# Attention pipeline of an encoder trunk: query turns moved two steps ahead, scores issued ahead of values, another first term, pieces at other steps

## The chip, the cores and the metric

The kernel is one program on 1 core of one Trainium2 chip. The metric is the device time of one execution in microseconds (us). Engines are named as in the profile: PE is TensorE's matmuls, PEld its weight loads, DVE is VectorE, ACT is ScalarE, POOL is GpSimd, SP is SyncE.

## The reference, cut to what matters

Two sequences of 512 and 256 tokens (768 in all, 6 blocks of 128) pass through two layers with shared weights. A layer is a half-weighted gated feed-forward, a mixer, and a second half-weighted feed-forward, each on a normalised input and each added to the running x. The mixer of layer 0 is a gated linear recurrence. The mixer of layer 1 is windowed attention with 16 query heads on 4 key heads, and the change is in this one:

```
qb = q.reshape(B, nb, L, Hk, G, d)                       # blocks of L=128 queries, G=4 heads per key head
s = einsum('bnqhgd,bnkhd->bnhgqk', qb, kband) * d**-0.5  # keys: the block, one before, one after
m = maximum(max(s), sink);  p = exp(s - m)
denom = sum(p) + exp(sink - m)
o = einsum('bnhgqk,bnkhd->bnqhgd', p / denom, vband)     # then o @ w_o
```

All inputs and outputs are float32. A product of float32 matrices is made of three products of the engine's faster float32 format: each operand is split into a high and a low part, and high*high, high*low and low*high are summed in PSUM.

## The kernel before, in words

**The whole.** `tile_trunk_kernel` runs feed-forward f0, the recurrence `hgrn`, feed-forwards f1 and f2, the attention `swa`, and f3. The products of the feed-forwards use a seven-product scheme for 2x2 blocks (L423, L498). Instructions are recorded in the order of the Python calls, and a scheduler then sets the order on each engine from that order, from the tiles that an instruction needs, and from when it reckons that these are ready. Each engine works through its own queue strictly in that order and waits on semaphores.

**The attention stage.** `swa` first projects keys and values for all blocks. The query projection is cut into pieces by the generator `proj_tok`: a query block of 512 columns takes 24 matmuls (L263, L264, L265) and is handed out in four pieces of six. After the fourth, `put_q` copies it out of PSUM (ACT, L970) and rotates 16 of every 64 columns (DVE, L973, L975, L976, L977). `q0` holds the queries of key heads 0 and 1, `q1` those of 2 and 3. Half of the output projection, `wo`, is cut into pieces in the same way.

**Units.** The attention is 24 units, numbered 0 to 23 here: 4 key heads, and for each the 6 query blocks, with all 4 query heads of one key head in a unit. Units with number 1 or 2 modulo 6 have three key blocks (384 keys), the others two (256 keys). A unit goes through these methods of `Unit`:

- `turn`: two PE transposes of the query block (L1155), then `split` into a high part by a copy on ACT (L268, tile tA) and a low part by a subtraction on DVE (L269, tile tA). The low part needs the high one.
- `scores`: 12 matmuls (L1169), three terms for each of 4 heads, with 64 of the 128 array rows each, two side by side; into 4 PSUM banks.
- `maxima`: four DVE instructions (L1185) that add the band mask and give the row maximum.
- `sink` and `exps`: DVE L1204; ACT exponentials with row sums (L1198) and that of the sink (L1205).
- `denominator`: DVE L1210, L1211, then the scaling of the four heads' probabilities (L1214).
- `probs`: per key block four PE transposes (L1221) and a copy by ACT (L1223, tile tA).
- `values`: matmuls (L1230) into 64 of the 128 array columns each; a source-level matmul here is two instructions on the engine.
- `finish`: a split of the result, ACT L268 and DVE L269 on tile big, the input of the output projection.

[...]

**What sets the order.** `pipeline` collects events with a step and a rank, sorts them by both, and calls them. Unit i has its section at step 4i: the matmuls of `values` of unit i-2 and of `scores` of unit i, tied into one chain with `issue_after`, then `finish` of unit i-2 and `maxima` of unit i. `turn` of unit i stands at step 4i-1 with rank 5 (the first at -5), the exponentials and the denominator at 4i with rank 2, the transposes of its probabilities at 4i+5 and on. The pieces come with rank 3 at the steps in the list `extra`: 16 query pieces (the last four blocks of `q0`), 25 more (`q1`), the reload of x, and 24 pieces of `wo`.

Of the kernel before, what the change touches and what calls it, by code (L numbers as in the profile page):

```python
# [48 lines left out]
class Trunk:  # L49
# [932 lines left out]
    def swa(self, next_row):  # L982
# [28 lines left out]
        def put_q(half):  # L1011
            def f(s, b, ps):
                gb = SEQS[s][0] // P + b
                if half and gb % 3 == 0:
                    hold.append(self.big([P, 3, 512]))
                t = hold[gb // 3][:, gb % 3] if half else self.xt()[:, :512]
                self.rotate(ps, 512 // HD, b, t.rearrange("p (h d) -> p h d", d=HD))
                for gg in range(2):
                    qtok[(s, b, half * 2 + gg)] = t[:, gg * 256 : (gg + 1) * 256]

            hold = []
            return f
# [3 lines left out]
        def units(gs):  # L1026
            def alloc(g):
                if g not in of:
                    of[g] = [self.big([P, 2, T], F32R) for _ in range(2)]
                return of[g]  # L1030

            for g in gs:
                for s, (off, n) in enumerate(SEQS):
                    for b in range(n // P):
                        q = lambda s=s, b=b, g=g: qtok[(s, b, g)]
                        yield Unit(self, s, b, g, q, kT, vv, lambda g=g: alloc(g))
# [4 lines left out]
        q = itertools.chain(self.proj_tok("q0", put_q(0)), self.proj_tok("q1", put_q(1)))  # L1041
        wo = self.out_proj("sw_o", 0, act, None)
        for _ in range(8):
            next(q)
        piece = lambda g: lambda: next(g, None)
        extra = [(i * 5 / 4 - 4, piece(q)) for i in range(16)]
        extra += [(18 + 2 * i, piece(q)) for i in range(25)]
        extra.append((46, self.reload_x))
        extra += [(66 + i * 5 / 4, piece(wo)) for i in range(24)]
        self.pipeline(list(units(range(KV))), extra)  # L1050
        self.drain(wo)
        self.drain(self.out_proj("sw_o", 1, act, next_row))
# [42 lines left out]
    def pipeline(self, units, extra):  # L1095
        events = []

        def at(step, rank, *calls):
            events.append((step, rank, len(events), calls))

        last = []

        def tiles(done, new):
            mms = ([] if done is None else done.values()) + ([] if new is None else new.scores())
            for n, mm in enumerate(mms):
                with self.tc.issue_after(last[-1]) if n else nullcontext():
                    last[:] = [mm()]

        def section(done, new):
            tiles(done, new)  # L1110
            if done is not None:
                done.finish()
            if new is not None:
                new.maxima()

        for i in range(len(units) + 2):
            t = 4 * i
            u = units[i] if i < len(units) else None
            done = units[i - 2] if i > 1 else None
            at(t, 1, lambda u=u, done=done: section(done, u))  # L1120
            if u is None:
                continue
            at(t - (1 if i else 5), 5, u.turn)
            at(t, 2, u.sink)
            for h in range(GQ):
                at(t, 2, lambda u=u, h=h: u.exps(h))
            at(t, 2, u.denominator)
            for j in range(u.nkb):
                at(t + 5 + j, 1, lambda u=u, j=j: u.probs(j))
        for step, call in extra:  # L1130
            at(step, 3, call)
        for _, _, _, calls in sorted(events, key=lambda e: e[:3]):
            for c in calls:
                c()


class Unit:
# [22 lines left out]
    def scores(self):  # L1160
        k, nc = self.k, self.k.nc
        self.sc = k.big([P, GQ, 3 * P])
        self.nm, self.den, self.sk = (k.stat(GQ) for _ in range(3))
        self.pss = [k.ps(self.nk) for _ in range(GQ)]

        def one(p, j, x, y, par):
            rows = slice(par * HD, (par + 1) * HD)
            q = self.qT[x][rows, p * P : (p + 1) * P]
            return nc.tensor.matmul(  # L1169
                self.pss[2 * p + par], q, self.kT[y][rows, self.keys], start=j == 0, stop=j == 2  # L1170
            ).ins

        terms = list(enumerate(((0, 0), (0, 1), (1, 0))))
        return [
            lambda p=p, j=j, x=x, y=y, par=par: one(p, j, x, y, par)
            for p in range(GQ // 2)
            for j, (x, y) in terms
            for par in range(2)
        ]
# [178 lines left out]
```

## Time and profile before

| what | value |
|---|---|
| time, median of 3 runs | 2759.03 us (2758.95 to 2759.92) |
| the profiled execution's own time | 2760.57 us |
| its span, first to last instruction | 2758.8 us |
| mean granted TensorE clock | 0.998 |
| busy share of the span: PE, DVE, ACT, POOL | 99%, 76%, 48%, 11% |
| first `scores` matmul to last `values` matmul | 2046.4 to 2226.2 us |

The profile of one execution has a page (engine totals, the span in 40 slices, the chain of work that ended last, the costliest groups of instructions) and views on the trace: the timeline of one engine in a stretch, tables of busy time by stretch, waits by who released whom. In a timeline row the first number is the start in us from the span's beginning, the second how long the row lasted; `x8` merges eight like instructions, and a bracket gives idle time of the engine ahead of the row and what ended it. PE matmuls overlap, so a matmul that "lasts" 0.39 us may be followed 0.23 us after its start by the next: the cost of a group on PE is read from its start to the start of the next group.

### The profile page before, as it was taken

To read this page: it belongs to the slowest core of one execution; us is meant where nothing else is said; L and a number is where in the kernel's file an instruction comes from. 1 tells how busy PE (TensorE), PEld (TensorE's weight loads), DVE (VectorE), ACT (ScalarE), POOL (GpSimd) and SP (SyncE) were. 2 spreads that over 40 slices of the span, in tenths; PEclk is the share of its full clock that TensorE was granted. 3 is DMA by queue.
4 is the path that set the end of the run, shared out by engine and by line. 5 is a ranking of instruction groups with operands and counts; after the bars stand their busy time and mean duration, and the time that the engine had idled before them with its cause. 6 is when DMAs were issued, how large, how long until landed. Compare 5 with 4: busy or idle time off the path is not lost.

```text
span 2758.8 us, 44483 instructions
## 1 busy us (share of the span) xinstructions
PE 2733.7 (99%) x17281; PEld 2481.9 (90%) x17281; DVE 2100.5 (76%) x3662; ACT 1327.5 (48%) x2479; POOL 309.2 (11%) x315
## 2 busy tenths in 40 slices
PE   8999999999999999999999999999999999999998
PEld 8999999888888889999999999999886789999997
DVE  7887788557477568787888878888846768788877
ACT  7444444456466354443446444444546654443444
POOL 1111211000000001121111112111000000221110
PEclk9999999999999999999999999999999999999999
DMA  5544554321110324455444355544412123555443
GB/s 161 135 117 118 137 135 118 120 64 41 55 46 25 122 62 109 118 143 135 120 120 106 88 127 138 134 116 120 151 43 77 47 62 81 134 136 130 117 115 107
DMA packets 330117, 291.63 MB, mean 106 GB/s; under 512 B 11609, under 2 KB 257841, under 8 KB 329905
## 3 DMA queue, kind: packets, MB, share of 16 engines
q1 hardware_dynamic: 294064, 212.43, 25.9%
q0 software_dynamic: 31680, 62.93, 13.3%
q10 hardware_dynamic: 4160, 13.42, 1.4%
q8 instruction: 135, 2.21, 0.3%
q14 instruction: 78, 0.63, 0.1%
HBM read 216.39 MB, written 9.44 MB: 82 GB/s over the span
## 4 chain that ended last, share of the span: by engine, by line
PE 95%; DVE 2%; ACT 2%; DMA 1%; issue 0%; DVEq 0%; SPq 0%; ACTq 0%
PE ps L423 41%; PE ps L498 20%; PE ps L263 9%; PE ps L265 9%; PE ps L264 9%; PE ps L694 1%; PE ps L1230 1%; PE ps L1169 1%; PE ps L839 1%; PE ps L1221 1%; PE ps L325 1%; DMA wr<-wr 1%; PE ps L815 0%; DVE x L520 0%; ACT big L328 0%
## 5 line engine op out<-in xcount | busy, mean ns | idle before, releaser
L423 PE MATMUL ps<-big,w 128*128 128x384 f32 x6720 | 1169.2, 334 | 0.0
L423 PEld LDWEIGHTS ps<-big,w 128*128 128x128 f32 x6720 | 1165.9, 188 | 1.6
L204 ACT CAST w<-wr 128x512 fp32r<-128x512 f32 x600 | 415.1, 706 | 707.4 <-DVE wr L218 371.6
L205 DVE TENSOR_TENSOR w<-wr,w 128x512 fp32r<-128x512 f32 (+1 forms) x520 | 448.5, 866 | 180.9 <-ACT w L204 176.0
L498 PE MATMUL ps<-w,big 128*128 128x512 f32 x2520 | 579.0, 390 | 2.0 <-DVE x L520 1.9
L498 PEld LDWEIGHTS ps<-w,big 128*128 128x128 f32 x2520 | 471.0, 188 | 104.8 <-ACT big L268 4.5
L520 DVE SCALAR_TENSOR_TENSOR x<-ps,x 128x512 f32<-128x512 f32 x468 | 303.6, 683 | 10.2 <-PE ps L265 10.0
L146 POOL DMA_DIRECT2D s<-wr x120 | 105.1, 875 | 1662.9 <-DMA wr<-in_ffn_w_dram 804.5
L263 PE MATMUL ps<-w,big 128*128 128x512 f32 x624 | 253.0, 405 | 0.3
L265 PE MATMUL ps<-w,big 128*128 128x512 f32 x624 | 244.8, 392 | 1.0 <-DVE big L332 1.0
L264 PE MATMUL ps<-w,big 128*128 128x512 f32 x624 | 244.8, 392 | 0.0
L268 ACT CAST big<-tA 128x384 fp32r<-128x384 f32 x296 | 148.1, 513 | 162.2 <-DVE tA L458 76.8
L263 PE MATMUL ps<-big,w 128*128 128x384 f32 (+2 forms) x640 | 219.2, 344 | 3.2 <-ACT big L268 1.9
L264 PE MATMUL ps<-big,w 128*128 128x384 f32 (+2 forms) x640 | 216.3, 338 | 0.7 <-DVE big L269 0.6
L265 PE MATMUL ps<-big,w 128*128 128x384 f32 (+2 forms) x640 | 215.5, 337 | 0.0
L269 DVE TENSOR_TENSOR big<-tA,big 128x384 fp32r<-128x384 f32 x296 | 183.9, 632 | 12.9 <-ACT big L268 12.0
L172 DVE TENSOR_TENSOR w<-wr,w 128x1024 fp32r<-128x1024 f32 x92 | 111.9, 1222 | 78.4 <-ACT w L171 72.6
L263 PEld LDWEIGHTS ps<-w,big 128*128 128x128 f32 x624 | 117.5, 188 | 29.3 <-issue 5.6
L205 POOL TENSOR_TENSOR w<-wr,w 128x512 fp32r<-128x512 f32 x80 | 123.3, 1541 | 179.7 <-ACT w L204 155.2
L171 ACT CAST w<-wr 128x1024 fp32r<-128x1024 f32 x92 | 96.5, 1052 | 97.3 <-PE ps L264 77.7
L265 PEld LDWEIGHTS ps<-w,big 128*128 128x128 f32 x624 | 117.4, 188 | 27.7 <-DVE big L332 1.7
L264 PEld LDWEIGHTS ps<-w,big 128*128 128x128 f32 x624 | 117.7, 189 | 21.8 <-issue 0.4
(163 smaller groups left out, 2906.6 us busy)
## 6 DMA issues: line engine op xcount, KB each, us to landing
wr<-in_ffn_w_dram SPq DMA_DIRECT2D x264, 512.0 KB, 3.9
s<-in_ffn_w_dram SPq DMA_DIRECT2D x120, 256.0 KB, 3.3
s<-wr POOLq DMA_DIRECT2D x120, 256.0 KB, 4.6
wr<-wr POOLq DMA_DIRECT2D x80, 256.0 KB, 3.7
wr<-in_hg_w_in_dram SPq DMA_DIRECT2D x40, 512.0 KB, 3.9
wr<-wr POOLq DMA_DIRECT2D x20, 512.0 KB, 4.6
spill<-x ACTq DMA_DIRECT2D x12, 512.0 KB, 2.8
x<-spill ACTq DMA_DIRECT2D x12, 512.0 KB, 3.3
```

The lines of the kernel that those rows point to most:

```text
L146: self.nc.gpsimd.dma_start(out, src, accum_op=ALU.add)
L172: self.nc.vector.tensor_sub(lo, raw, hi.bitcast(F32))
L204: nc.scalar.copy(h, src)
L205: low = (eng or nc.vector).tensor_sub(l, src, h.bitcast(F32)).ins
L263: nc.tensor.matmul(out, a[0], b[0], start=first, stop=False)
L264: nc.tensor.matmul(out, a[0], b[1], start=False, stop=False)
L265: nc.tensor.matmul(out, a[1], b[0], start=False, stop=last)
L268: self.nc.scalar.copy(hi, src)
L269: self.nc.vector.tensor_sub(lo, src, hi.bitcast(F32))
L423: self.nc.tensor.matmul(ps, a[x], b[y], start=first and k == 0 and i == 0, stop=k == 3 and i == 2, skip_group_check=True,)
L498: nc.tensor.matmul(ps, a[x], w[y], start=name == chain and kp == 0 and q == 0, stop=kp == 1 and q == 2, skip_group_check=True,)
L520: self.nc.vector.scalar_tensor_tensor(x, ps, c, x, ALU.mult, ALU.add)
```

## The change

Five edits, all in the attention stage:

1. `turn` of unit i moves from step 4i-1 (rank 5) to step 4i-2 (rank 2).
2. In a section the chain begins with `scores` of the new unit and ends with `values` of the old one, and `maxima` is called before `finish`.
3. In `scores` the term order of (query part, key part) is low*high, high*high, high*low; it was high*high, high*low, low*high. So the first matmul of a unit needs the low part of the query.
4. The first 16 query pieces stand 7/5 of a step apart (5/4 before), the next 25 begin at step 19 (18 before).
5. The 24 pieces of `wo` stand 7/5 of a step apart (5/4 before).

```diff
-        extra = [(i * 5 / 4 - 4, piece(q)) for i in range(16)]
-        extra += [(18 + 2 * i, piece(q)) for i in range(25)]
+        extra = [(i * 7 / 5 - 4, piece(q)) for i in range(16)]
+        extra += [(19 + 2 * i, piece(q)) for i in range(25)]
         extra.append((46, self.reload_x))
-        extra += [(66 + i * 5 / 4, piece(wo)) for i in range(24)]
+        extra += [(66 + i * 7 / 5, piece(wo)) for i in range(24)]
...
-            mms = ([] if done is None else done.values()) + ([] if new is None else new.scores())
+            mms = ([] if new is None else new.scores()) + ([] if done is None else done.values())
...
             tiles(done, new)
+            if new is not None:
+                new.maxima()
             if done is not None:
                 done.finish()
-            if new is not None:
-                new.maxima()
...
-            at(t - (1 if i else 5), 5, u.turn)
+            at(t - (2 if i else 5), 2, u.turn)
...
-        terms = list(enumerate(((0, 0), (0, 1), (1, 0))))
+        terms = list(enumerate(((1, 0), (0, 0), (0, 1))))
```

What the scheduler makes of it is seen at three places. **First, PE between unit 11 and unit 13.** Before, the turn of unit 12 (L1155), the values of unit 10 (L1230), three projection matmuls, and the first seven of the twelve score matmuls of unit 12 (L1169):

```order
L1155 MATMUL ps_2723_20272<-ident_r_84,big_2625_19823 128x128 x2
L1230 MATMUL ps_2725_20278<-tA_2714_20245,big_2447_18825 64x256 x2
L1230 MATMUL ps_2725_20278<-tA_2716_20252,big_2447_18825 64x256 x2
L263 MATMUL ps_2701_20178<-w_2576_19601,big_2422_18734 128x512
L264 MATMUL ps_2701_20178<-w_2577_19602,big_2422_18734 128x512
L265 MATMUL ps_2701_20178<-w_2576_19601,big_2422_18734 128x512
L1169 MATMUL ps_2730_20283<-big_2445_18823,tA_2724_20275 128x256
L1169 MATMUL ps_2731_20284<-big_2445_18823,tA_2724_20275 128x256
L1169 MATMUL ps_2730_20283<-big_2446_18824,tA_2724_20275 128x256
L1169 MATMUL ps_2731_20284<-big_2446_18824,tA_2724_20275 128x256
L1169 MATMUL ps_2730_20283<-big_2445_18823,tA_2724_20275 128x256
L1169 MATMUL ps_2731_20284<-big_2445_18823,tA_2724_20275 128x256
```

Now the end of the score matmuls of unit 12, the values of unit 10, the transposes of unit 11 (L1221), the turn of unit 13, and the first three of the fifteen projection matmuls that end at the scores of unit 13:

```order
L1169 MATMUL ps_2731_20284<-big_2446_18824,tA_2718_20257 128x256
L1169 MATMUL ps_2732_20285<-big_2446_18824,tA_2718_20257 128x256
L1230 MATMUL ps_2733_20286<-tA_2714_20239,big_2447_18825 64x256 x2
L1230 MATMUL ps_2733_20286<-tA_2716_20252,big_2447_18825 64x256 x2
L1221 MATMUL ps_2734_20321<-ident_r_84,big_2704_20191 128x128 x4
L1221 MATMUL ps_2738_20341<-ident_r_84,big_2704_20191 128x128 x4
L1155 MATMUL ps_2740_20348<-ident_r_84,big_2627_19830 128x128 x2
L263 MATMUL ps_2742_20354<-w_2563_19551,big_2416_18728 128x512
L264 MATMUL ps_2742_20354<-w_2564_19552,big_2416_18728 128x512
L265 MATMUL ps_2742_20354<-w_2563_19551,big_2416_18728 128x512
```

Scores, values, transposes and the turn now stand in one stretch, and the projection in another. Counted over the stage, PE goes from one kind of work to another 157 times, where it was 190, with the same number of matmuls of each kind. Between the start of the scores of one unit and of the next there are now 9 or 8 projection matmuls in some sections and 15 or 16 in others.

**Second, DVE after the maxima of unit 11.** Before: `sink` (L1204) and the denominator of unit 11, the low part of the query of unit 12 (tA_2724), the scaling of unit 11 (L1214), the finish of unit 10 (tile big_2659), the first maximum of unit 12:

```order
L1204 TENSOR_TENSOR stat_2708_20195<-stat_2706_20193,nsinks_202 128x4
L1210 TENSOR_TENSOR stat_2707_20194<-stat_2707_20194,stat_2708_20195 128x4
L1211 RECIPROCAL stat_2707_20194<-stat_2707_20194 128x4
L269 TENSOR_TENSOR tA_2724_20275<-ps_2723_20272,tA_2724_20275 128x256
L1214 TENSOR_SCALAR big_2705_20192<-big_2705_20192,stat_2707_20194 128x256 x4
L269 TENSOR_TENSOR big_2659_19958<-ps_2725_20278,big_2658_19957 128x2x128
L1185 ISA big_2726_20279,stat_2727_20280<-ps_2730_20283,big_2442_18818,nsinks_202 128x256
```

Now the same engine and place, where tA_2718 is the low part of the query of unit 12 and big_2659 the finish of unit 9:

```order
L1204 TENSOR_TENSOR stat_2707_20194<-stat_2705_20192,nsinks_202 128x4
L269 TENSOR_TENSOR big_2659_19962<-ps_2712_20199,big_2658_19961 128x2x128
L1210 TENSOR_TENSOR stat_2706_20193<-stat_2706_20193,stat_2707_20194 128x4
L1211 RECIPROCAL stat_2706_20193<-stat_2706_20193 128x4
L1214 TENSOR_SCALAR big_2704_20191<-big_2704_20191,stat_2706_20193 128x256 x4
L269 TENSOR_TENSOR tA_2718_20257<-ps_2717_20254,tA_2718_20257 128x256
L1185 ISA big_2725_20278,stat_2726_20279<-ps_2729_20282,big_2442_18818,nsinks_202 128x256
```

The low part of the next unit's query has gone from ahead of the scaling of this unit to behind it. Counted over the stage, the low part of the next unit stood ahead of the scaling behind 12 of the 23 units that have a successor; now it does behind two, units 1 and 16.

**Third, DVE where the sixth query block of `q0` is rotated (tile x, L973 to L977).** Before, behind the scaling of unit 3 and a split of weights (L172), ahead of the low part of the query of unit 4 (tA_2584):

```order
L1214 TENSOR_SCALAR big_2558_19513<-big_2558_19513,stat_2560_19515 128x256 x4
L172 TENSOR_TENSOR w_2577_19602<-wr_2488_19134,w_2576_19601 128x1024
L973 TENSOR_TENSOR x_2579_19607<-ps_2551_19493,big_2442_18818 128x8x16
L975 TENSOR_TENSOR tB_2580_19610<-ps_2551_19493,big_2442_18818 128x8x8
L976 TENSOR_TENSOR tB_2580_19610<-ps_2551_19493,big_2442_18818 128x8x8
L269 TENSOR_TENSOR tA_2584_19624<-ps_2583_19621,tA_2584_19624 128x256
L977 TENSOR_TENSOR x_2579_19607<-x_2579_19607,tB_2580_19610 128x8x16
```

Now behind the scaling of unit 4 and a split of weights, ahead of the low part of the query of unit 5 (tA_2599), whose turn needs this very block:

```order
L1214 TENSOR_SCALAR big_2580_19608<-big_2580_19608,stat_2582_19610 128x256 x4
L172 TENSOR_TENSOR w_2592_19667<-wr_2488_19134,w_2591_19666 128x1024
L973 TENSOR_TENSOR x_2594_19672<-ps_2562_19544,big_2442_18818 128x8x16
L975 TENSOR_TENSOR tB_2595_19675<-ps_2562_19544,big_2442_18818 128x8x8
L976 TENSOR_TENSOR tB_2595_19675<-ps_2562_19544,big_2442_18818 128x8x8
L977 TENSOR_TENSOR x_2594_19672<-x_2594_19672,tB_2595_19675 128x8x16
L269 TENSOR_TENSOR tA_2599_19689<-ps_2598_19686,tA_2599_19689 128x256
```

The rotation has moved back by a whole unit against the sections.

## The prediction

> **What bounds the kernel now.** I read the page first: the span, the engine totals and the chain of work that ended last.
>
> ```profile
> span 2758.8 us, 44483 instructions
> ...
> PE 2733.7 (99%) x17281; PEld 2481.9 (90%) x17281; DVE 2100.5 (76%) x3662; ACT 1327.5 (48%) x2479; POOL 309.2 (11%) x315
> ...
> PE 95%; DVE 2%; ACT 2%; DMA 1%; issue 0%; DVEq 0%; SPq 0%; ACTq 0%
> ```
>
> The page's PE entry is at 99%, and the chain is PE for 95% of the span. The time is that of PE's queue, so an edit to its order pays only as far as it removes idle time there or makes a group of matmuls shorter. The edits touch one stage, so next came the table of busy time for it and for a part of it, then PE's timeline where that part has a hole.
>
> ```profile
> 2040.00:2230.00 190.00, 187.85 (x1188) 137.03 (x1187) 130.47 (x477) 116.67 (x344) 0.00 (x0) 0.99 0.16 51
> ...
> 2080.60:2083.90 3.30, 3.30 (x13) 2.91 (x12) 1.34 (x7) 2.26 (x8) 0.00 (x0) 0.50 0.35 126
> ```
>
> ```profile
> 2076.60 0.65 PE L1230 MATMUL ps<-tA,big 128*64 128x256 f32 x4 [0.51 <-ACT tA L1223]
> 2078.40 0.65 PE L1230 MATMUL ps<-tA,big 128*64 128x256 f32 x4 [1.15 <-ACT tA L1223]
> 2078.99 0.50 PE L1169 MATMUL ps<-big,tA 64*128 64x256 f32 x4
> 2079.64 0.74 PE L1169 MATMUL ps<-big,tA 64*128 64x256 f32 x8 [0.16 <-DVE tA L269]
> ```
>
> PE is idle for 190.00 - 187.85 = 2.15 us in the whole stage, and 0.51 + 1.15 + 0.16 = 1.82 us of it is here, at unit 4. Behind it the granted clock is 0.50 for the 3.3 us of the second row, which costs another half of that, 1.7 us. Elsewhere the stage is full: DVE and ACT have 60 to 75 us to spare in total, but the question for this change is when they deliver.
>
> **What PE's own work costs.** Read from start to start, in an undisturbed unit, then scores with 384 keys, values that scores follow directly, long values, and a turn that projection follows:
>
> ```profile
> 2130.86 0.38 PE L1155 MATMUL ps<-ident_r,big 128*128 128x128 f32 x2
> 2131.17 1.08 PE L1230 MATMUL ps<-tA,big 128*64 128x256 f32 x8
> 2132.19 0.50 PE L263 MATMUL ps<-w,big 128*128 128x512 f32 x1
> 2132.52 0.40 PE L264 MATMUL ps<-w,big 128*128 128x512 f32 x1
> 2132.76 0.39 PE L265 MATMUL ps<-w,big 128*128 128x512 f32 x1
> 2133.08 0.98 PE L1169 MATMUL ps<-big,tA 64*128 64x256 f32 x12
> 2133.99 0.50 PE L263 MATMUL ps<-w,big 128*128 128x512 f32 x1
> 2134.32 0.40 PE L264 MATMUL ps<-w,big 128*128 128x512 f32 x1
> 2134.56 0.39 PE L265 MATMUL ps<-w,big 128*128 128x512 f32 x1
> 2134.79 1.03 PE L1221 MATMUL ps<-ident_r,big 128*128 128x128 f32 x8
> 2135.58 0.48 PE L263 MATMUL ps<-w,big 128*128 128x512 f32 x1
> ...
> 2182.68 1.31 PE L1169 MATMUL ps<-big,tA 64*128 64x384 f32 x12
> 2183.93 0.50 PE L263 MATMUL ps<-w,big 128*128 128x512 f32 x1
> ```
>
> ```profile
> 2166.80 1.08 PE L1230 MATMUL ps<-tA,big 128*64 128x256 f32 x8
> 2167.81 0.97 PE L1169 MATMUL ps<-big,tA 64*128 64x256 f32 x12
> ...
> 2150.85 1.52 PE L1230 MATMUL ps<-tA,big 128*64 128x256 f32 x12
> ...
> 2158.27 0.38 PE L1155 MATMUL ps<-ident_r,big 128*128 128x128 f32 x2
> 2158.41 0.47 PE L264 MATMUL ps<-w,big 128*128 128x512 f32 x1
> ```
>
> Scores cost 0.91 us (256 keys) or 1.25 (384), values 1.02 (two blocks) or 1.45 (three: the row's 1.52 less the 0.07 by which the short ones' 1.08 runs over), eight transposes 0.79, a turn 0.31 ahead of values. A projection matmul follows the last after 0.23 us (2134.32 to 2134.56), but the first of a run takes 0.33, and the last ahead of a tiled group 0.32 (2132.76 to 2133.08).
>
> **Term 1, fewer changes of kind: -4.5 us.** Runs of projection matmuls go from 72 to 45 in the order of the stage: 27 times the 0.10 us of a first one, -2.7. A turn stands directly ahead of values 17 times before and never after; against a turn ahead of projection (2158.27 to 2158.41, 0.14) that is 0.17 each, -2.9. Four units no longer have scores in two parts and four no longer have values in two parts, about 0.2 us each time (0.33 + 0.32 - 2 x 0.23), together -1.4. Against this transposes and turns follow each other or a tiled group more often, some 36 times, at 0.06 to 0.08 by the spread of such rows (an estimate from 0.31 against 0.14 for a turn, shared by its two matmuls), +2.5. What the trace never shows is values behind scores, now 22 times. I take the 0.91 of scores ahead of projection with nothing added, as scores add nothing behind values (1.01 against 1.02); the bounds are that and the 0.09 that a tiled group costs behind projection, so 0 to +2.0.
>
> **Term 2, the hole at unit 4: -3.5 us.** The values there wait for probabilities copied late (L1223). In the new order a unit's values stand a whole section behind its transposes, so these 1.82 us and the 1.7 of clock go. What is late next is the scores.
>
> **Term 3, scores wait for the low part: +10.2 us.** The first score matmul now needs the low part of the query, and DVE makes that behind the scaling of the unit before. The scaling closes a chain that starts at that unit's scores. Unit 23 shows the chain nearly free of others, on PE, DVE and ACT; then the ends of units 19 (scores at 2182.68, above) and 2:
>
> ```profile
> 2216.37 0.98 PE L1169 MATMUL ps<-big,tA 64*128 64x256 f32 x12
> ...
> 2217.23 0.47 DVE L1185 CUSTOM_DVE_ANT_0 big<-ps,big,nsinks 128x256 f32<-128x256 f32 x1
> ...
> 2217.75 0.51 ACT L1198 ACTIVATE big<-big,stat 128x256 f32<-128x256 f32 x1 [0.89 <-DVE stat L1185]
> ...
> 2220.26 0.49 ACT L1198 ACTIVATE big<-big,stat 128x256 f32<-128x256 f32 x1
> ...
> 2220.87 0.16 DVE L1210 TENSOR_TENSOR stat<-stat,stat 128x4 f32<-128x4 f32 x1 [1.15 <-ACT big L1198]
> ...
> 2221.28 1.14 DVE L1214 TENSOR_SCALAR big<-big,stat 128x256 f32<-128x256 f32 x4
> ```
>
> ```profile
> 2188.46 1.41 DVE L1214 TENSOR_SCALAR big<-big,stat 128x384 f32<-128x384 f32 x4
> ```
>
> ```profile
> 2059.51 1.31 PE L1169 MATMUL ps<-big,tA 64*128 64x384 f32 x12
> ...
> 2066.47 1.41 DVE L1214 TENSOR_SCALAR big<-big,stat 128x384 f32<-128x384 f32 x4
> ...
> L269 DVE TENSOR_TENSOR tA<-ps,tA 128x256 fp32r<-128x256 f32 x24 | 9.8, 408 | 0.5 <-ACT tA L268 0.5
> ```
>
> From the first score matmul to the end of the scaling: 2222.42 - 2216.37 = 6.05 us for 256 keys, 2189.87 - 2182.68 = 7.2 for 384, and 8.4 for unit 2 with copies in ACT's way. With the subtraction behind it (0.41, of which some 0.07 runs beside the last scaling) the next scores can start 6.4, 7.5 and 8.7 us after these. PE's own way from scores to scores in the new order, for unit 11 with nine projection matmuls: 0.91 + 1.02 + 0.79 + 0.31 + (9 x 0.23 + 0.19) = 5.3, so it lacks 1.1. For units 7 and 13 (384 keys, the same row of work) 5.6, lacking 1.9 each. In the same way, with the matmuls that the order has in each section: unit 2 lacks 3.1 (its way is 5.6 against 8.7), 9 and 15 lack 0.5 each (eight projection matmuls, long values, twelve transposes: 5.9), 19 lacks 1.2 (twice six projection matmuls: 6.3). Sum: 10.2. Sections with 12 to 16 projection matmuls take 6.4 to 7.6 and lack nothing. No wait carries over, since each chain starts at the scores that it held up. Queued behind the waiting matmul are the values, transposes and the next turn, all of PE.
>
> **Term 4, turns wait for the rotation: +6.6 us.** The sixth block of `q0` is rotated on DVE behind the scaling of unit 4, and the turn of unit 5 needs it a few steps later. On DVE:
>
> ```profile
> L172 DVE TENSOR_TENSOR w<-wr,w 128x1024 fp32r<-128x1024 f32 x92 | 111.9, 1222 | 78.4 <-ACT w L171 72.6
> ...
> L975 DVE TENSOR_TENSOR tB<-ps,big 128x64 f32<-128x64 f32 x11 | 2.4, 216 | 0.0
> ...
> L977 DVE TENSOR_TENSOR big<-big,tB 128x128 f32<-128x128 f32 x6 | 1.7, 291 | 0.2
> ```
>
> From the scores of unit 4: 6.05, one split of weights (1.14 beyond its overlap) between its maxima and another behind its scaling, and the four rotating instructions, 0.85: 9.2 us. PE's way to the turn: scores 0.91, values 1.45, eight transposes in two parts 0.9, six projection matmuls 1.5, 4.7 us. It waits 4.5. The same block of `q1`, for unit 17: first maximum 1.4 us behind the scores of unit 16 because of a split, three more 1.2, another split 1.14, the finish, the sink and the rotation 1.7, 5.4 in all; PE is at the turn after 0.91 + 1.45 + 0.9 = 3.3. It waits 2.1.
>
> **Term 5, the clock behind the long waits: +8.5 us.** The 1.82 us of idle time at unit 4 were followed by 3.4 us at half clock. Terms 3 and 4 have five waits of 1.9 to 4.5 us; each at 1.7 is 8.5. Some may fall in two or hide in a section with time to spare, some may bring two drops: 3 to 8 drops, 5 to 13.6 us. [...]
>
> The order of the terms and the spacing of the pieces cost nothing beyond these: the number of matmuls, copies and DMAs is the same, and the loads of the next weights stand in the same order on SP's queue. The reload of x on ACT's queue follows the same pieces as before.
>
> **Sum.** -4.5 - 3.5 + 10.2 + 6.6 + 8.5 = +17.3 us. The profiled execution took 2760.57 us, 1.8 more than its span and 1.5 more than the median of the runs, so 2777.9 for such a one and 2776 against the median of 2759.03. 0.2% of it is 5.5 us, about what a measurement of this kernel can tell from no change.
>
> **The rivals.** [...] Chance 0.15. (b) The waits are as reckoned, values behind scores cost the 0.09 each and eight drops come: +2.0 + 5.1, 2783 us. For it that several waits are just long enough. Chance 0.11. (c) The chain is a microsecond shorter in the new order, since maxima no longer stand behind a finish and exponentials may begin at once: term 3 falls to some 4.3, term 4 to 4.5, two drops remain, 3.4; -8.0 + 12.2 = +4, 2763 us, no change that can be told. For it that in unit 23 ACT idles between its first and second exponential; against it that unit 23 is already the free case. Chance 0.08. (d) Faster: DVE delivers the low part before PE gets there. It decides at a chain of 5.3 us for 256 keys and 5.6 for 384: below it nothing but terms 1 and 2 is left, and with the blocks rotated in time the kernel takes 2759.0 - 8.0 = 2751 us. For it that the order of the scheduler gives PE's queue fewer changes, and that DVE is busy for only 130 of the stage's 190 us; against it the rows 2216.37 to 2221.28. Chance 0.06. That the edits do nothing is out: the order has moved on PE, DVE and ACT.
>
> **How the numbers follow.** The forecast has 0.60: 2776 us. Slower by over 0.2% takes in the forecast, (a) and (b), 0.86; within 0.2% is (c), 0.08; faster by over 0.2% is (d), 0.06. The range: low, (c) at 2763; high, (b) at 2783 and 2 us for short waits in the sections not listed, 2785. It leaves out (d) and the tails of the others.
>
> **What would show it.** Right: in the stage's waits, scores (L1169) behind the low part (DVE tA L269) with about 10 us, two turns (L1155) behind a rotation (L977) with 4.5 and 2; five or so stretches of 3.4 us at clock 0.50 between 2070 and 2220; the hole of the values at unit 4 gone; scores in one piece everywhere; values 1.0 us long behind scores. Wrong: PE's table of busy time as full as before, scores starting 5.3 us after the last ones, or a granted clock of 1.0 throughout with the waits there.

## The result, and the profile after

| | before | after |
|---|---|---|
| time, median | 2759.48 us (2758.15 to 2762.06, 6 runs) | 2776.18 us (2775.73 to 2777.41, 6 runs) |
| the profiled execution | 2760.57 us | 2775.73 us |
| its span | 2758.8 us | 2774.0 us |

The ratio is 1.0062, with a 95% interval of 1.0050 to 1.0073: the change makes the kernel slower by 0.6%, 16.7 us. The forecast was 2776 us.

The page after, with the totals of the engines and the chain that ended last:

```profile
span 2774.0 us, 44406 instructions
...
PE 2733.9 (99%) x17281; PEld 2485.2 (90%) x17281; DVE 2102.2 (76%) x3662; ACT 1329.4 (48%) x2479; POOL 310.0 (11%) x315
...
PE 94%; DVE 3%; ACT 2%; issue 0%; DMA 0%; DVEq 0%; SPq 0%; ACTq 0%
```

Totals hardly tell the two kernels apart: PE's busy time moved by 0.2 us, and the chain has one percent more on DVE. The stage does. First the same 1188 PE instructions that filled 190.00 us before, then pieces of 3.41 us, cut where the granted clock changes. The columns are the length, busy time (and instructions) of PE, PEld, DVE, ACT and POOL, then the granted clock, the DMA share and GB/s:

```profile
2040.00:2246.00 206.00, 188.65 (x1188) 141.08 (x1187) 132.64 (x477) 115.04 (x344) 0.00 (x0) 0.95 0.14 45
2065.98:2069.39 3.41, 0.74 (x12) 0.74 (x12) 2.85 (x12) 2.02 (x6) 0.00 (x0) 1.00 0.00 0
2069.39:2072.80 3.41, 3.41 (x18) 1.66 (x16) 1.79 (x9) 0.88 (x4) 0.00 (x0) 0.50 0.00 0
2083.04:2086.46 3.42, 0.27 (x3) 0.03 (x1) 2.12 (x7) 2.99 (x9) 0.00 (x0) 1.00 0.44 151
2086.46:2093.28 6.82, 5.38 (x24) 3.96 (x26) 2.87 (x11) 0.37 (x1) 0.00 (x0) 0.50 0.24 79
...
2171.79:2175.20 3.41, 1.67 (x19) 1.25 (x20) 3.06 (x9) 3.33 (x6) 0.00 (x0) 1.00 0.43 145
2175.20:2178.62 3.42, 3.39 (x16) 2.05 (x12) 3.42 (x14) 0.96 (x2) 0.00 (x0) 0.50 0.51 153
```

PE is idle for 206.00 - 188.65 = 17.35 us of the stage, where it was 2.15. Six stretches of 3.41 us are at half clock (the row of 6.82 us holds two, and those from 2113.76 and 2158.14 aren't shown), where there was one. Together they hold 20.5 us, of which 1.46 are idle; half of the other 19.0 us, 9.5, is lost to the clock, by the estimate that PE's work takes twice as long there (long values took 2072.41 - 2069.66 = 2.75 us from start to start in the first of them, and 1.45 at clock 1.00 in the kernel before), and 1.7 was before. In the waits of the stage (us in total, times, longest) stands whom PE waits for:

```profile
PE ps L1169 <- DVE tA L269: 12.2, 8, 3.1
...
PE ps L1155 <- DVE x L977: 4.6, 1, 4.6
```

With 0.5 us of a second turn these are the waits that were forecast, and there is no other: values no longer wait for copied probabilities (L1223). One by one, on PE's timeline, with the idle time ahead of the row in the bracket:

```profile
2068.64 1.08 PE L1169 MATMUL ps<-big,tA 64*128 64x256 f32 x12 [3.05 <-DVE tA L269]
2087.89 0.66 PE L1155 MATMUL ps<-ident_r,x 128*128 128x128 f32 x2 [4.59 <-DVE x L977]
2113.47 2.06 PE L1169 MATMUL ps<-big,tA 64*128 64x384 f32 x12 [1.89 <-DVE tA L269]
2129.04 0.98 PE L1169 MATMUL ps<-big,tA 64*128 64x256 f32 x12 [0.47 <-DVE tA L269]
2142.53 0.98 PE L1169 MATMUL ps<-big,tA 64*128 64x256 f32 x12 [1.16 <-DVE tA L269]
2156.67 1.34 PE L1169 MATMUL ps<-big,tA 64*128 64x384 f32 x12 [1.89 <-DVE tA L269]
2173.60 0.98 PE L1169 MATMUL ps<-big,tA 64*128 64x256 f32 x12 [1.74 <-DVE tA L269]
2179.14 0.41 PE L1155 MATMUL ps<-ident_r,big 128*128 128x128 f32 x2 [0.55 <-DVE big L977]
2204.45 1.33 PE L1169 MATMUL ps<-big,tA 64*128 64x384 f32 x12 [1.19 <-DVE tA L269]
2214.91 0.98 PE L1169 MATMUL ps<-big,tA 64*128 64x256 f32 x12 [0.82 <-DVE tA L269]
```

They are the scores of unit 3, the turn of unit 5, the scores of units 8, 10, 12, 14 and 16, the turn of unit 17, the scores of units 20 and 21. How one comes about is seen at unit 12. PE's rows from the scores of unit 11 to the transposes, and the last matmul ahead of the wait:

```profile
2136.07 0.97 PE L1169 MATMUL ps<-big,tA 64*128 64x256 f32 x12
2136.97 1.08 PE L1230 MATMUL ps<-tA,big 128*64 128x256 f32 x8
2137.99 1.09 PE L1221 MATMUL ps<-ident_r,big 128*128 128x128 f32 x8
...
2140.99 0.39 PE L265 MATMUL ps<-w,big 128*128 128x512 f32 x1
```

The chain beside it, the first maximum and the end on DVE, then the high part of unit 12 on ACT:

```profile
2136.72 0.48 DVE L1185 CUSTOM_DVE_ANT_0 big<-ps,big,nsinks 128x256 f32<-128x256 f32 x1 [1.34 <-PE ps L1169]
...
2141.00 1.14 DVE L1214 TENSOR_SCALAR big<-big,stat 128x256 f32<-128x256 f32 x4
2142.05 0.42 DVE L269 TENSOR_TENSOR tA<-ps,tA 128x256 fp32r<-128x256 f32 x1
```

```profile
2141.40 0.38 ACT L268 CAST tA<-ps 128x256 fp32r<-128x256 f32 x1
```

PE is through with the section at 2141.38, 5.3 us after it began; DVE ends the scaling 6.07 us after that beginning and the low part at 2142.47, and the scores begin 0.06 us later. The high part, which the low one needs, was there at 2141.78, 0.27 us before the low part began. Values behind scores cost 2137.99 - 2136.97 = 1.02 us, as they did elsewhere, and the scores ahead of them 0.90.

### The profile page after: what moved, and what is told of

It is laid out like the page before. It is cut to its first block, busy times and chain, and to the rows that moved or that the text cites. A ratio compares the mean times of both kernels' runs of the same rounds, so it can differ in the third digit from the quotient of the medians.

```text
span 2774.0 us, 44406 instructions
## 1 busy us (share of the span) xinstructions
PE 2733.9 (99%) x17281; PEld 2485.2 (90%) x17281; DVE 2102.2 (76%) x3662; ACT 1329.4 (48%) x2479; POOL 310.0 (11%) x315
## 4 chain that ended last, share of the span: by engine, by line
PE 94%; DVE 3%; ACT 2%; issue 0%; DMA 0%; DVEq 0%; SPq 0%; ACTq 0%
PE ps L423 42%; PE ps L498 20%; PE ps L263 9%; PE ps L265 8%; PE ps L264 8%; PE ps L694 1%; PE ps L1230 1%; PE ps L1169 1%; PE ps L839 1%; PE ps L1221 1%; PE ps L325 1%; ACT big L1198 1%; PE ps L815 0%; DVE x L520 0%; DVE w L172 0%
## 5 line engine op out<-in xcount | busy, mean ns | idle before, releaser
L520 DVE SCALAR_TENSOR_TENSOR x<-ps,x 128x512 f32<-128x512 f32 x468 | 304.2, 686 | 10.1 <-PE ps L265 10.0
L269 DVE TENSOR_TENSOR big<-tA,big 128x384 fp32r<-128x384 f32 x296 | 184.2, 633 | 12.8 <-ACT big L268 11.6
L172 DVE TENSOR_TENSOR w<-wr,w 128x1024 fp32r<-128x1024 f32 x92 | 111.9, 1223 | 80.0 <-ACT w L171 72.6
L265 PEld LDWEIGHTS ps<-w,big 128*128 128x128 f32 x624 | 117.4, 188 | 26.9 <-DVE big L332 1.7
```

The lines of the kernel that those rows point to most:

```text
L172: self.nc.vector.tensor_sub(lo, raw, hi.bitcast(F32))
L265: nc.tensor.matmul(out, a[1], b[0], start=False, stop=last)
L269: self.nc.vector.tensor_sub(lo, src, hi.bitcast(F32))
L520: self.nc.vector.scalar_tensor_tensor(x, ps, c, x, ALU.mult, ALU.add)
```

## The experiments

Each was timed beside the kernel before on the same chip (its medians there: 2759.44 to 2759.89 us). The first, third, fourth and fifth undo edits of the change in the kernel after (one each, the fifth two); the second makes one of them alone in the kernel before. A bracket behind a ratio is its 95% interval.

**Values ahead of scores again.** Edit 2 is undone, the other four stay.

```diff
-            mms = ([] if new is None else new.scores()) + ([] if done is None else done.values())
+            mms = ([] if done is None else done.values()) + ([] if new is None else new.scores())
...
-            if new is not None:
-                new.maxima()
             if done is not None:
                 done.finish()
+            if new is not None:
+                new.maxima()
```

> The changed kernel with values ahead of scores again and finish ahead of maxima (edit 2 undone, the rest kept). Theory (scores ahead of values is what leaves the next unit's low part behind this unit's chain): the low part stands ahead of the scaling behind 12 of 23 units again, the 12.2 us that PE spent idle on it fall below 1, and with them three or four of the six stretches at half clock; the turn of unit 5 still waits some 3 us for its rotation, so one or two stretches stay. About 10 us below the changed kernel, 2766 (2763 to 2770). Rival (the earlier turn is what puts the low part behind): no more than 3 us below, 2773 to 2777.

2766.08 us, ratio to the kernel before 1.0023 (1.0014 to 1.0033): 10.1 us less than after. In DVE's order the low part of the next unit is again ahead of the scaling behind 12 of 23 units, as before the change. In the stage's waits of PE no row of scores behind L269 is left. Beside 1.4 us of transposes there are the two turns, 2.7 us (unit 5) and 3.7 (unit 17), and three stretches at half clock:

```profile
PE ps L1155 <- DVE big L977: 3.7, 1, 3.7
...
PE ps L1155 <- DVE x L977: 2.7, 1, 2.7
```

**Scores ahead of values alone.** The same edit, made alone in the kernel before.

```diff
-            mms = ([] if done is None else done.values()) + ([] if new is None else new.scores())
+            mms = ([] if new is None else new.scores()) + ([] if done is None else done.values())
...
-            if done is not None:
-                done.finish()
             if new is not None:
                 new.maxima()
+            if done is not None:
+                done.finish()
```

> The kernel before the change with edit 2 alone: scores ahead of values, maxima ahead of finish. Theory: this edit alone sends the low part behind the scaling behind all but 4 units and brings waits of the scores, the long ones at units 4 and 16, some 8 to 12 us in all, and one to three stretches of half clock, against 4 to 5 us saved on changes of kind and the hole of unit 4: 4 to 9 us slower than before, 2763 to 2768. Rival (it takes edit 1 or 3 to do harm): faster than before by 3 to 8 us, 2751 to 2756.

2766.91 us, 1.0026 (1.0016 to 1.0037). The low part is ahead of the scaling behind 4 units only. The high part is the first term here, so the scores wait for ACT's copy as well:

```profile
PE ps L1169 <- ACT tA L268: 6.9, 6, 3.1
```

and 1.9 us for the low part in five places.

Edit 2 alone makes the kernel 7 us slower, and there are three half-clock stretches. With the experiment ahead of it: it is this edit that sends the split of the query behind the chain, not the earlier step of the turn. The forecast had not said which of the edits does.

**The turn at its old step.** Edit 1 is undone.

```diff
-            at(t - (2 if i else 5), 2, u.turn)
+            at(t - (1 if i else 5), 5, u.turn)
```

> The changed kernel with the turn at its old step (edit 1 undone). Theory: the waits of the scores stay, since the order of scores and values is kept (the low part is ahead of the scaling behind only 2 of 23 units); the waits of the two turns, 4.6 and 0.5 us, go, and a wait of the scores of unit 5 and a longer one of unit 16 come in their place. Within 4 us of the changed kernel, 2771 to 2777. Rival (the earlier turn is to blame): the waits of the scores go as well, 12 us and four stretches of half clock, 2757 to 2762.

2772.21 us, 1.0044 (1.0029 to 1.0059), 4.0 less than after. The scores' waits for the low part are longer: 16.5 us in ten places, the longest 3.5. The turns, a step later, have their rotated block and wait for nothing, and four stretches are at half clock. So the earlier turn shortens the scores' waits by 4 us, and costs more than that at units 5 and 17.

**The high part first.** Edit 3 is undone.

```diff
-        terms = list(enumerate(((1, 0), (0, 0), (0, 1))))
+        terms = list(enumerate(((0, 0), (0, 1), (1, 0))))
```

> The changed kernel with the old order of terms (edit 3 undone): the low part is needed by the fifth score matmul and no longer by the first. Theory: PE starts on the high part, some 0.4 us before the low one is there, and needs it for the third pair only 0.2 us later, so each of eight waits gets shorter by 0.5 to 0.9, and some end too short to bring the clock down: 4 to 8 us below the changed kernel, 2768 to 2772, with the wait of the turn of unit 5 unchanged at 4.6. Rival (the chain ends at the high part anyway, which ACT makes behind the exponentials): less than 2 us, 2774 to 2777.

2771.02 us, 1.0041 (1.0026 to 1.0056), 5.2 less than after. The scores begin on the high part and wait for the rest in the middle of a group:

```profile
PE ps L1169 <- ACT tA L268: 3.1, 4, 1.4
...
PE ps L1169 <- DVE tA L269: 2.1, 7, 0.5
```

5.2 us in place of 12.2, and the waits of scores bring no half clock any more: its three stretches stand behind the turns of units 5 and 17 (4.7 and 1.9 us).

**The pieces at their old steps.** Edits 4 and 5 are undone.

```diff
-        extra = [(i * 7 / 5 - 4, piece(q)) for i in range(16)]
-        extra += [(19 + 2 * i, piece(q)) for i in range(25)]
+        extra = [(i * 5 / 4 - 4, piece(q)) for i in range(16)]
+        extra += [(18 + 2 * i, piece(q)) for i in range(25)]
...
-        extra += [(66 + i * 7 / 5, piece(wo)) for i in range(24)]
+        extra += [(66 + i * 5 / 4, piece(wo)) for i in range(24)]
```

> The changed kernel with the pieces at their old steps (edits 4 and 5 undone). Theory: the turn of unit 5 finds its block rotated, so its 4.6 us go with one or both of the two stretches of half clock behind it; the turn of unit 17 still waits, some 2 us; the scores wait as in the changed kernel, about 10 us. 5 to 9 us below the changed kernel, 2767 to 2771. Rival (the wait moves on to the scores of unit 5, which hang on the same DVE queue): less than 2 us, 2774 to 2777.

2768.56 us, 1.0034 (1.0022 to 1.0045), 7.6 less than after. The turn of unit 5 waits no more, that of unit 17 for 2.3 us; scores wait 9.2 us in six places, and three stretches are at half clock. Undone in these four steps, the edits give back 10.1 + 4.0 + 5.2 + 7.6 = 26.9 us of a loss of 16.7, so their costs overlap. Undoing edit 2 and undoing edit 3, for instance, shorten the same waits of scores, from 12.2 us to none and to 5.2.

**The scaling later.** The kernel after, with the denominator and the scaling recorded two steps later, so that the low part might come ahead of it again.

```diff
-            at(t, 2, u.denominator)
+            at(t + 2, 2.5, u.denominator)
```

> The changed kernel with one line different: the denominator of a unit is called at step 4i+2 and rank 2.5, so behind the turn of the next unit, and the scheduler leaves the low part ahead of the scaling behind 13 of 23 units (2 in the changed kernel). Theory as the prediction had it (DVE's place behind the scaling is what the scores wait for): where the low part goes ahead, the wait shrinks by the scaling's 1.1 to 1.4 us, 12.2 us in all fall to about 4, 8 to 12 us below the changed kernel, 2764 to 2768. Rival (the high part, made by ACT behind the exponentials and two copies, is as late as the scaling, so DVE's order is only the last link): the waits shrink by 0.3 to 0.6 us each, 2 to 5 us below, 2771 to 2774.

2769.05 us, 1.0036 (1.0023 to 1.0049): 7.1 less than after, between what the two theories gave, and outside both ranges. The edit did less than was meant. The scaling of a unit is four instructions, and on DVE's timeline the low part stands ahead of all four behind unit 15 alone; behind 12 units it stands among them, in seven of them ahead of the last one only, and behind ten it follows them. (The 13 units of the expectation are those where it is ahead of the last.) Scores still wait 8.1 us in eight places, where it was 12.2:

```profile
PE ps L1169 <- DVE tA L269: 8.1, 8, 1.8
```

The turn of unit 17 waits 2.8 us where it waited 0.5, so the waits fell by some 2 us in all. Three stretches are at half clock, three fewer than after, and that is worth some 5 us, most of the gain.

What else holds the scores up? The low part needs the high one, and that copy stands in ACT's queue behind the exponentials and two copies of probabilities. Unit 14, on ACT, DVE and PE:

```profile
2147.94 1.04 ACT L1223 COPY tA<-ps 128x512 f32<-128x512 f32 x2
2148.88 0.37 ACT L268 CAST tA<-ps 128x256 fp32r<-128x256 f32 x1
```

```profile
2148.47 1.08 DVE L1214 TENSOR_SCALAR big<-big,stat 128x384 f32<-128x384 f32 x3
2149.47 0.42 DVE L269 TENSOR_TENSOR tA<-ps,tA 128x256 fp32r<-128x256 f32 x1
```

```profile
2149.94 1.34 PE L1169 MATMUL ps<-big,tA 64*128 64x384 f32 x12 [1.55 <-DVE tA L269]
```

PE was free at 2148.39 and the high part was there at 2149.25. The low part followed three scaling instructions without a gap, so DVE's queue still set its start. Had it begun right behind the high part, PE would still have waited some 1.4 of the 1.55 us: 0.86 for the high part, 0.42 for the subtraction and about 0.06 on either side of it. The same estimate for the kernel after, from the ends of its high parts, leaves 7.9 us of the 11.4 in seven of its eight waits; the eighth, unit 21's, would go. So each theory was right in part, and the first only about the last link: in the kernel after DVE's scaling ends the waits, but ACT's queue stands right behind it and would hold PE for about two thirds of that time. Unit 16 bears this out, the one whose low part went ahead of the whole scaling: 0.79 us of its wait are left, where the kernel after waits 1.74. No run takes the scaling out of the way in all units at the change's step of the turn, so the two thirds stay an estimate.

**Work put into the waits.** The kernel after, with 51 matmuls of 512 columns added, whose results nobody reads: 12 ahead of the scores of unit 3, 7 each ahead of those of units 8, 14 and 16, 18 ahead of the turn of unit 5.

```diff
-            mms = ([] if new is None else new.scores()) + ([] if done is None else done.values())
+            mms = fill(self, new, FILL) + ([] if new is None else new.scores()) + ([] if done is None else done.values())
...
-        k = self.k
+        k = self.k; [mm() for mm in fill(k, self, FILL_TURN)]
...
+FILL, FILL_TURN = {3: 12, 8: 7, 14: 7, 16: 7}, {5: 18}
+def fill(k, u, table):
+    n = table.get(u.g * 6 + u.off // P + u.b, 0) if u else 0
+    if not n:
+        return []
+    ps, keys = k.ps(), u.kT[0][:, :512]
+    return [lambda: k.nc.tensor.matmul(ps, k.identr, keys, start=True, stop=True).ins] * n
```

> The changed kernel with 51 matmuls of 128x512 added whose result nobody reads: 12, 7, 7 and 7 ahead of the scores of units 3, 8, 14 and 16 and 18 ahead of the turn of unit 5, each stretch a little shorter (0.23 us a matmul) than the wait there. Theory (PE's idle time brings the clock down, 1.7 us for each of the six stretches at half clock): added work makes it faster, by 6 to 10 us, 2766 to 2770, with at most one stretch of half clock left in the stage and the waits of the scores and the turn nearly gone from the timeline. Rival (the stretches of half clock hide in waits that would be there anyway): no faster, 2776 to 2779.

2770.08 us, 1.0037 (1.0024 to 1.0050): 6.1 us *faster* than after, with more work in it. The whole stage, then two pieces around the turn of unit 17, which waits 2.10 us here:

```profile
2040.00:2240.00 200.00, 192.43 (x1242) 145.76 (x1241) 132.49 (x477) 115.20 (x344) 0.00 (x0) 1.00 0.16 48
2167.57:2170.99 3.42, 2.69 (x24) 1.65 (x22) 3.42 (x11) 2.21 (x5) 0.00 (x0) 1.00 0.43 111
2170.99:2174.40 3.41, 2.04 (x10) 1.76 (x11) 2.38 (x13) 2.41 (x11) 0.00 (x0) 1.00 0.67 193
```

The clock is 1.00 for the whole stage, although this wait alone is longer than three of those that brought half clock in the kernel after; its stretches hold 0.73 and 1.37 us of idle time. PE's idle time fell by 17.35 - 7.57 = 9.8 us, the added matmuls take 51 x 0.23 = 11.7, and the 9.5 us of half clock are gone: -7.6, and the span fell by 6.2. The work put in is longer than the waits that it filled; what made the kernel faster is the clock.

**The turn earlier still.** Scores ahead of values and the low part first, as after; but the turn goes to step 4i-4, and the query pieces to where its blocks are ready by then. `wo` is at its old steps.

```diff
-        extra = [(i * 7 / 5 - 4, piece(q)) for i in range(16)]
-        extra += [(19 + 2 * i, piece(q)) for i in range(25)]
+        extra = [(i - 4, piece(q)) for i in range(16)]
+        extra += [(14 + 2 * i, piece(q)) for i in range(25)]
...
-        extra += [(66 + i * 7 / 5, piece(wo)) for i in range(24)]
+        extra += [(66 + i * 5 / 4, piece(wo)) for i in range(24)]
...
-            at(t - (2 if i else 5), 2, u.turn)
+            at(t - (4 if i else 5), 1, u.turn)
```

> Scores ahead of values and the low part first, as in the changed kernel, but the turn of a unit at step 4i-4 and rank 1, right behind the section of the unit before, the pieces at steps i-4 and 14+2i, those of the output projection as before the change. Theory: both parts of the query are split before the exponentials and the scaling of the unit before (ahead of the scaling behind all 23), so no scores wait for them; the blocks are rotated in time; what is left is the PE order with fewer changes of kind, 4 to 5 us, and the hole of unit 4 gone, 3.5 us. 4 to 8 us below the kernel before the change, 2751 to 2755, and no stretch of half clock in the stage. Rival (the chain from scores to scaling bounds a unit whatever stands behind it, by making the transposes of the probabilities late instead): no better than before, 2759 to 2765.

2753.72 us, 0.9978 (0.9969 to 0.9987): it beats both kernels. The low part is ahead of the scaling behind all 23 units. The stage, and the low part of unit 12 with its scores:

```profile
2040.00:2230.00 190.00, 187.67 (x1214) 139.83 (x1213) 129.55 (x478) 117.48 (x344) 0.00 (x0) 1.00 0.16 51
```

```profile
2127.73 0.41 DVE L269 TENSOR_TENSOR tA<-ps,tA 128x256 fp32r<-128x256 f32 x1
...
2130.97 1.14 DVE L1214 TENSOR_SCALAR big<-big,stat 128x256 f32<-128x256 f32 x4
```

```profile
2129.88 0.98 PE L1169 MATMUL ps<-big,tA 64*128 64x256 f32 x12
```

The low part ended at 2128.14, the scores begin at 2129.88 without a bracket: no wait. PE is idle for 2.33 us of the 190, and no stretch is at half clock.

**The same pieces without the earlier turn.** To tell the turn from the pieces, the experiment above with the turn at the change's step:

```diff
-            at(t - (4 if i else 5), 1, u.turn)
+            at(t - (2 if i else 5), 2, u.turn)
```

> The pieces of the experiment with the early turn (query pieces one step apart, the next 25 from step 14, wo as before), with the turn at the step that the change gave it; scores ahead of values, low part as first term. Theory (what costs is the low part behind the scaling, which only an earlier turn mends): the low part stands ahead of the scaling behind only 4 of the 23 units, the waits of scores stay, 7 to 12 us; the waits of the turns for the rotation go; 1 to 3 stretches of 3.4 us at half clock: 2763 to 2768 us. Rival (the pieces alone made the early turn's gain, by where projection matmuls stand between scores): waits of scores below 3 us, no half clock, 2753 to 2757 us.

2764.47 us, 1.0017 (1.0008 to 1.0027). The low part is ahead of the scaling behind 4 units, scores wait 10.7 us in eight places, no turn waits, and one stretch is at half clock. The longest of these waits, 2.82 us, is unit 15's, whose low part stands ahead of the whole scaling: the high part, behind the exponentials on ACT, came at 2156.47, 2.31 us after PE was free. So it isn't enough to have the low part ahead of the scaling; both parts must be early. Of the 22.5 us between after and the version with the early turn, the pieces account for 11.7 and the turn's step, taken after them, for 10.7.

**Values first with the early turn.** The version with the early turn, with edit 2 undone as in the first experiment.

> The experiment with the early turn, with values ahead of scores and the finish ahead of the maxima, as before the change. Theory (scores ahead of values are a gain once the low part is early, since values then have a whole section's time to get their probabilities): scores wait for nothing, values wait for the copies of probabilities by some 2 to 4 us, one stretch at half clock perhaps: 2755 to 2760 us, 2 to 6 us above the one with scores first. Rival (the order of the two is indifferent once the turn is early): 2752 to 2755 us.

2762.84 us, 1.0013 (1.0003 to 1.0022). The direction is the theory's, the size isn't: 9.1 us over the version with scores first, where 2 to 6 were expected. Values wait for their probabilities by 6.4 us in six places, the longest 2.5, not 2 to 4; transposes wait another 3.1 us for DVE, and one stretch is at half clock.

Four kernels now make a table (us):

| | turn at step 4i-2, pieces of the change | turn at step 4i-4, earlier pieces |
|---|---|---|
| values first | 2766.08 | 2762.84 |
| scores first | 2776.18 | 2753.72 |

The same edit, scores ahead of values, costs 10.1 us in one column and gains 9.1 in the other.

## Why the prediction was right, and where its terms were off

From the first instructions of the stage to the last values PE takes 15.9 us longer than before. The span grew by 15.2; the 0.7 between them lies outside the stage.

**Term 1 (fewer changes of kind): forecast -4.5, measured -7.1.** I added up the time from each group's start to the next group's start over the stage, without waits and without what half clock added:

| PE time, us | projection | turns | scores | values | transposes | sum |
|---|---|---|---|---|---|---|
| before | 98.5 | 6.2 | 26.1 | 28.8 | 22.9 | 182.6 |
| after | 95.7 | 3.8 | 24.3 | 27.6 | 24.2 | 175.5 |

Projection (-2.8 for -2.7) and turns (-2.5 for -2.9) were sized well. Scores and values gave back 3.0, not the 1.4 reckoned for split groups. Who follows a group isn't the reason: a whole group of scores with 256 keys takes 0.92 us ahead of projection (before) and 0.91 ahead of values (after). Of the other 1.6, 0.7 lies at unit 4, whose groups, broken by waits, took 0.4 and 0.3 us longer than whole ones, and so belongs to the hole of term 2; 0.5 lies in three more groups of scores of the kernel before; and some 0.3 comes from halving the time at half clock in the kernel after. The +2.5 for transposes and turns among themselves came to +1.2. Values behind scores, the one cost that no trace had shown, add nothing: the value taken (0) held, and its upper bound of +2.0 is out.

**Term 2 (the hole at unit 4): right.** Its waits of values are gone, and the scores are what is late next, as the prediction said.

**Term 3 (scores wait for the low part): forecast 10.2, measured 12.2.** Seven of the eight waits were named, with 3.1, 1.9, 0.5, 1.1, 1.9, 0.5 and 1.2; six of them measure 3.05, 1.89, 0.47, 1.16, 1.89 and 1.19. The seventh, unit 16's, was forecast at 0.5 and took 1.74: ACT copies probabilities and the finish ahead of the first exponential of unit 15, whose maxima were done at 2168.27.

```profile
2168.38 0.37 ACT L268 CAST big<-ps 128x256 fp32r<-128x256 f32 x1 [2.10 <-PE ps L1230]
2168.96 0.59 ACT L1223 COPY tA<-ps 128x512 f32<-128x512 f32 x1 [0.20 <-PE ps L1221]
2169.44 0.51 ACT L1198 ACTIVATE big<-big,stat 128x256 f32<-128x256 f32 x1
```

The eighth, unit 21's 0.82 us, was not on the list: "Sections with 12 to 16 projection matmuls take 6.4 to 7.6 and lack nothing" held for the scaling, but DVE has two splits of weights between scaling and low part there.

```profile
2212.16 2.36 DVE L172 TENSOR_TENSOR w<-wr,w 128x1024 fp32r<-128x1024 f32 x2
```

The order showed both: the chain is as long as what is queued inside it, on both engines. The term also took DVE's scaling for the whole cause. It is the last link, but ACT's high part is only 0.3 to 1.0 us ahead of it in the seven waits named, so a shorter DVE queue alone would have saved some 3.5 of 11.4 us (the estimate under "The scaling later").

**Term 4 (turns wait for the rotation): forecast 4.5 + 2.1, measured 4.59 + 0.55.** The rotation of the second came 5.4 us after the scores of unit 16, as reckoned (2178.99 against 2173.60). PE's own way to the turn was 5.0 us and not 3.3, because it went at half clock:

```profile
2174.50 2.19 PE L1230 MATMUL ps<-tA,big 128*64 128x256 f32 x12
2176.62 1.97 PE L1221 MATMUL ps<-ident_r,big 128*128 128x128 f32 x8
```

That stretch of half clock, counted in term 5, took the place of a wait: the two were added in the forecast, and share their time on the chip.

**Term 5 (the clock): forecast five stretches, 8.5; measured six, 9.5.** Against before this is +7.8 where 8.5 - 1.7 = 6.8 was forecast. The sixth stands behind the wait of 4.59 us, which left 3.15 us idle in one stretch and 1.44 in the next; each of the two was followed by one at half clock.

**In sum:** waits 17.35 - 2.15 = +15.2 (forecast 16.8 - 1.8 = 15.0), clock +7.8 (6.8), fewer changes -7.1 (-4.5), together +15.9 for +17.3. The median moved by 16.7. That the forecast hit within a microsecond is in part luck: a larger gain in term 1 met a larger loss to the clock, and the waits agree to 0.2 us because term 3 was 2.0 too low and term 4 was 1.5 too high.

**The rivals.** (a), 2770 us with one drop of the clock in place of five, is out, and no run shows it: in the kernel after the granted clock was 0.50 behind waits of 1.74, 1.89 and 1.89 us as well as behind those of 3.05 and 4.59, and the experiment with added matmuls took away the half clock and 6.1 us with it. (b) is out with values at no extra cost and six stretches, not eight. (c), a chain shorter by a microsecond, is out: 6.07 us at unit 11 where 6.05 was reckoned. (d) didn't happen in this kernel; what it needed, the low part ahead of PE, is what the version with the early turn brings, 2753.72 us for the 2751 that (d) gave.

## What to carry to other kernels

When an edit puts a consumer ahead on a full engine, look at where its producer stands in the other engines' in-order queues: here the same edit was worth -9 or +10 us, depending on whether the split of the next query, a copy on ACT and a subtraction on DVE of 0.4 us each, stood ahead of a chain of 6 us or behind it. Work out, section by section, the engine's own way round against the chain's way round, with everything that is queued inside the chain on each engine; the difference is the wait, to 0.1 us in six of eight cases here. And weigh waits on PE by the clock they may cost, not only by their length: here 9.5 us of clock went with 17.35 us of idle time.

## What the runs showed of the hardware

**In these traces the clock went by the idle time within fixed stretches, not by the length of one wait.** The granted clock changes on a grid of 3.413 us: in the kernel after it falls at 2069.39, 2086.46, 2113.76, 2158.14 and 2175.20 us, and these are 5, 8, 13 and 5 such steps apart. I cut all twelve traces of the stage on their grids. Of 23 stretches with 1.7 us or more of idle PE, 22 were followed by one at half clock; of the 14 between 1.3 and 1.7 us, 4 were, and two of these 4 stood at half clock already; of those at full clock with less, none was. A stretch at half clock needed less to be followed by another: all five with 0.77 us or more of idle time were, and none of the 23 with 0.17 us or less. In the kernel before, the three short waits at unit 4 fell into one stretch:

```profile
2077.10:2080.52 3.42, 2.11 (x20) 1.24 (x19) 3.42 (x13) 1.89 (x5) 0.00 (x0) 1.00 0.58 180
```

That is 1.31 us of idle time, and half clock followed. With the pieces of the early turn but not the turn, a single wait of 2.82 us was followed by no half clock; an edge cut it into 1.34 and 1.47:

```profile
2152.09:2155.51 3.42, 2.08 (x13) 1.48 (x11) 2.62 (x4) 3.26 (x10) 0.00 (x0) 1.00 0.54 163
2155.51:2158.92 3.41, 1.94 (x22) 1.52 (x24) 2.64 (x10) 2.76 (x8) 0.00 (x0) 1.00 0.64 232
2158.92:2162.33 3.41, 2.25 (x22) 1.63 (x18) 3.41 (x14) 2.67 (x9) 0.00 (x0) 1.00 0.04 14
```

So here it mattered where the edges fell against the program, and the count of half-clock stretches was forecast only roughly, five for six. What exactly is counted stays open: 1.31 us were enough once, and 1.91 us once were not, in a stretch whose only work was twelve transposes (values first with the early turn).

**Unread matmuls made this kernel faster.** 11.7 us of them took the half clock away and 6.1 us off the time; no stretch of that kernel's stage has more than 1.4 us of idle time. The better cure was to take the waits away: 22.5 us.
